# A tuned streaming-encoder layer: low parts of weight blocks kept in DRAM, and score products of both heads in one chain of turns at given places

## The chip, the cores and the metric

The kernel runs on one core of one Trainium2 chip. The metric is the device time of one execution in microseconds, the median of several runs. Five engines work side by side, each through its own queue of instructions in a fixed order: TensorE (PE in the profile), VectorE (DVE), ScalarE (ACT), GpSimd (POOL) and SyncE (SP), which here issues DMAs only. An instruction waits at the head of its engine's queue until its semaphores have come, and all behind it wait too.

## What is computed

One layer on x of 2048 tokens by 1024 features, in float32. h is the normed x, one product with w_in gives the columns of attention, of the recurrent mixer (RWKV-7) and of two gates, and a feed-forward network follows. Cut to what matters here:

```python
proj = h @ w_in[l]
p_att, p_rwkv = proj[..., :ATT_COLS], proj[..., ATT_COLS:ATT_COLS + RWKV_COLS]
p_gate = proj[..., ATT_COLS + RWKV_COLS:] + gate_bias[l]
...
def step(state, inp):
    r_t, w_t, k_t, v_t, aa_t, bb_t = inp
    sa = jnp.einsum('bhij,bhj->bhi', state, aa_t)
    state = (state * w_t[:, :, None, :] + sa[..., None] * bb_t[:, :, None, :]
             + v_t[..., None] * k_t[:, :, None, :])
    y = jnp.einsum('bhij,bhj->bhi', state, r_t)
    return state, y
...
merged = gate_a * (y_a @ proj_a[l]) + gate_b * (y_b @ proj_b[l])
x = x + rms_norm(merged @ w_out[l], post_mix_g[l])
u = jnp.square(jax.nn.relu(hf @ w_up[l])) @ w_down[l]
x = x + rms_norm(u, post_ffn_g[l])
```

There are 8 recurrent heads of 64 features. The kernel does not run the recurrence token by token: it takes chunks of 64 tokens, makes products of all tokens of a chunk with each other (the scores, ps_A), inverts a triangular matrix for each chunk, and carries the state from chunk to chunk.

## The kernel before

The tokens are taken in four groups of 512. Each group goes through `phase_rwkv` (recurrent mixer and gates), `phase_attention` and `phase_merge`; then the feed-forward network runs in two halves. Groups are counted from 0.

**Dense blocks.** A block of 128 columns of w_in is one call of `dense` (L118): the raw block of 512 KB comes on SP (`load_raw`, L64), ScalarE makes its high part whi (L81) and VectorE its low part wlo = raw - whi (L83), both through `wsplit`, with two buffers each. 24 products of 128x512 follow into one bank (psd, L92): eight each of hh x whi, hl x whi and hh x wlo. So the low part is used last. `phase_rwkv` has 30 such blocks a group: 14 of the mixer (columns 12 to 25 of w_in, counted in blocks) and 16 of the gates (26 to 41). The first two blocks of group 0 have their low part made on GpSimd. `follow`, just ahead of it, orders the split behind the emptying of an earlier bank.

**The recurrent stage.** Four pairs of heads, p = 0 to 3, in two batches of two. `rwkv_pre` prepares a pair: r, k, v from dense blocks; ps_z and ps_a (L428, L429) for decay and rate; ps_v, ps_bonus and ps_bk; then the scores. The eight chunks go in two halves of four. Each half takes two banks of PSUM, one for each head (`both`), from a pool of two buffers that ps_z, ps_a, ps_v, ps_bonus, ps_bk and ps_t share. Per chunk and head there is one product (L585). VectorE then empties each bank with four instructions: two into NA (L596), one into AR (L602) and one into BR (L603). NA holds what is to be inverted for two pairs.

`rwkv_inverse` works on VectorE alone: NA is transposed into N (L611), 31 steps of T (L621) and X (L627) follow, and X is transposed (L630) into X1 and XD (L632). `rwkv_blocks` starts TensorE on the result (ps_t, L652 and L660); `rwkv_trans` makes ps_at, ps_w, ps_ug, ps_tq and ps_s, with TQ (L713, L716) and S (L724) by VectorE; `rwkv_chunk` carries the state: ps_st and ps_y on TensorE (L738, L742), ST or, at the last chunk, st on VectorE (L743). `rwkv_post` norms the result: var on VectorE (L756), two steps on GpSimd that end in grs (L757, L759), yn on VectorE (L761). The chunks of the first two pairs run beside the preparation of the other two.

**The order of the work.** A scheduler fills each engine's queue from the program and from the dependences. `queue_behind` adds an order without a wait. The list `self.dl` holds the dense products of the group's `phase_rwkv` in turn (30 x 24), and `place(mm, n)` puts a product behind the n-th of them. Before the change only the first score product of the first pair has a place (SCORES = 150); where the others come is left to the scheduler.

Of the kernel before, what the change touches and what calls it, by code (L numbers as in the profile page):

```python
# [9 lines left out]
F32 = mybir.dt.float32  # L10
BF16 = mybir.dt.bfloat16
F32R = mybir.dt.float32r
# [4 lines left out]
DRAM = bass.MemoryType.DRAM  # L17

P = 128
D = 1024  # L20
KB = D // P
# [15 lines left out]
TURNED = 438  # L37
FIFTH = 494
BONUS = {(0, 1): 138, (1, 0): 258}
SCORES = 150  # L40
TURNS = {1: (588, 592)}
DEC = math.exp(-0.5)

ATT0 = 0
# [12 lines left out]
class Block:  # L57
# [54 lines left out]
    def follow(self):  # L112

        for ins, done in zip((self.high.ins, self.low), self.emptied[-3] if len(self.emptied) > 2 else ()):
            if done is not None:
                self.queue_behind(ins, done.ins)

    def dense(self, col):  # L118

        first = bool(self.raws)  # L120
        wh, wl = self.wsplit(self.w_in(col), "w", KB, P, lower=self.nc.gpsimd if first else None)
        if first:
            n = 1 - len(self.raws)
            self.queue_behind(self.high.ins, self.highs[n])
        self.follow()
        ps = self.pd.tile([P, G], F32, tag="d", name="psd")
        terms = [(wh[:, k], wl[:, k], self.h[0][:, k], self.h[1][:, k]) for k in range(KB)]
        if first:
            pairs = [(u, h) for u, _, h, _ in terms] + [(v, h) for _, v, h, _ in terms] + [(u, l) for u, _, _, l in terms]
            self.mm = [  # L130
                self.nc.tensor.matmul(ps, l, r, start=n == 0, stop=n == len(pairs) - 1).ins
                for n, (l, r) in enumerate(pairs)
            ]
            self.queue_behind(self.mm[0], self.last_transpose)
        else:
            self.mm = self.mm3(ps, terms, True)
        self.dl += self.mm
        return ps
# [19 lines left out]
    def constants(self, ctx, mixing):  # L158
        tc, nc, a = self.tc, self.nc, self.a
        keep = ctx.enter_context(tc.tile_pool(name="const", bufs=1))  # L160
        cp = mixing.enter_context(tc.tile_pool(name="mconst", bufs=1, side="right"))
        dp = ctx.enter_context(tc.tile_pool(name="scratch", bufs=1, space=DRAM))
        nrow = sum(n for _, n in ROWS)
        self.cst = cp.tile([P, nrow], F32, name="cst")
        nc.sync.dma_start(self.cst, a["cst"])
# [279 lines left out]
    def rwkv_pre(self, g, p, rp, NA, between=lambda: None):  # L445
        nc = self.nc
        pc = slice(p * P, (p + 1) * P)
        col = slice(p, p + 1)
# [17 lines left out]
        between()  # L466
        nc.vector.tensor_scalar(tw, tw, -0.5 * DEC, -0.5 * DEC, ALU.mult, ALU.add)
        cum = tw
# [84 lines left out]
        for i, x in enumerate((rh, rl)):  # L553
            mm = nc.tensor.matmul(psb, self.bones, x, start=i == 0, stop=i == 1)
# [22 lines left out]
        for h in range(2):  # L577
            cs = slice(h * 4, h * 4 + 4)

            both = [self.pa.tile([P, 4, P], F32, tag="a", name="ps_A") for _ in range(2)]  # L580
            for j in range(4):
                c = h * 4 + j
                for par, psA in enumerate(both):
                    rw = slice(par * C, par * C + C)
                    mm = nc.tensor.matmul(  # L585
                        psA[:, j].rearrange("p (s t) -> p s t", t=C),
                        BK[rw, c].rearrange("p s t -> p (s t)"),
                        AR[rw, c, par : 3 : 2 - par], start=True, stop=True,
                    )
                    if p == c == par == 0:  # L590
                        self.place(mm, SCORES)
            for par, psA in enumerate(both):
                ow = slice(C - par * C, P - par * C)
                for lo, w in ((0, C), (32, 32)):
                    hw = slice(par * C + lo, par * C + lo + 32)
                    nc.vector.tensor_tensor(  # L596
                        NA[hw, q, cs, 0:w],
                        psA[hw, :, lo : lo + w],
                        n2[hw, cs, par, None].to_broadcast((32, 4, w)),
                        ALU.mult,  # L600
                    )
                nc.vector.tensor_tensor(AR[ow, cs, par], psA[ow, :, 0:C], mS[ow], ALU.mult)  # L602
                nc.vector.tensor_tensor(BR[:, cs, par, 1], psA[:, :, C:P], mN[:, par, cs], ALU.mult)  # L603
# [144 lines left out]
    def rwkv_post(self, p, R):  # L748
# [18 lines left out]
        for h in range(2):  # L767
            ps = self.pr.tile([C, 4, P], F32, tag="wus", name="ps_yt")
            for j in range(4):
                mm = nc.tensor.transpose(ps[:, j], yn[:, h * 4 + j], self.ident)  # L770
                if j == 0 and p in TURNS:
                    self.place(mm, TURNS[p][h])
            cs = slice(h * 4, h * 4 + 4)
# [876 lines left out]
```

## Time and profile before

| | us |
|---|---|
| median of 3 runs | 3199.82 (3198.31 to 3202.85) |
| profiled execution, its own time | 3198.07 |
| its span on the core | 3196.4 |
| TensorE busy | 3147.3 (98%) |
| VectorE busy | 2235.8 (70%) |
| ScalarE busy | 1578.7 (49%) |
| GpSimd busy | 613.8 (19%) |

The mean granted clock of TensorE is 0.999. A row of a timeline is a run of like instructions: start, duration from its first start to its last end, engine, line, operation, tiles (written<-read), shapes and count; in brackets the idle time ahead of it and what ended it. TensorE's instructions overlap, so the time that a run costs is read from its start to the next one's. The trace counts two instructions for a score product. A row of a group has busy time and mean ns of one behind the first bar, and idle time with its releasers behind the second. A row of waits has the waiting engine, tile and line, what it waited for, and total us, times and the longest. A window row has its length, then busy time and count of PE, PEld, DVE, ACT and POOL, the clock, the share of the DMA engines and GB/s.

### The profile page before, as it was taken

The page shows a single profiled execution, that of the slowest core. Times are in us where ns is not written, and L with a number is a line of the kernel's source. Part 1 is how long each engine was busy: PE and PEld are TensorE (multiplying, and loading weights), DVE is VectorE, ACT ScalarE, POOL GpSimd, SP SyncE. Part 2 cuts the span into 40 slices and gives each one's busy share as a digit, 9 for nine tenths or more (in the row PEclk, how much of TensorE's full clock was granted, in tenths as well). Part 3 has the DMA queues.
Part 4 walks back from the last instruction along what each step waited for, and adds up shares of the span by engine and source line. Part 5 has one row for each costly group of instructions (what it writes and reads, how often), then busy time and mean ns, then how long its engine had stood idle before and what let it go on. Part 6 is the DMA issues. An engine that isn't in the chain of part 4 may idle for free. (4 is left out here: it accounts for less than half of the span.)

```text
span 3196.4 us, 49803 instructions
## 1 busy us (share of the span) xinstructions
PE 3147.3 (98%) x18800; PEld 2575.3 (81%) x18800; DVE 2235.8 (70%) x3668; ACT 1578.7 (49%) x2511; POOL 613.8 (19%) x1119
## 2 busy tenths in 40 slices
PE   8999999999999999999999999999999999999998
PEld 6877788778888877888877888888888878888887
DVE  6785667776767786767876776877656768765564
ACT  5435645445745445745534755454544454444343
POOL 3222012132112222112222101221211112210000
PEclk9999999999999999999999999999999999999999
DMA  6245473157573246574236466554877866547565
GB/s 192 86 135 189 134 259 129 60 172 244 175 260 129 77 141 245 186 235 160 94 116 228 160 208 261 192 179 162 293 268 251 281 225 213 170 156 244 191 221 174
DMA packets 197477, 598.82 MB, mean 187 GB/s; under 512 B 25570, under 2 KB 25708, under 8 KB 197236
## 3 DMA queue, kind: packets, MB, share of 16 engines
q1 hardware_dynamic: 139124, 415.24, 40.1%
q0 software_dynamic: 48896, 163.61, 13.6%
q10 hardware_dynamic: 9216, 16.78, 1.4%
q8 instruction: 148, 2.42, 0.3%
q14 instruction: 93, 0.76, 0.1%
HBM read 431.67 MB, written 167.01 MB: 187 GB/s over the span
## 5 line engine op out<-in xcount | busy, mean ns | idle before, releaser
L1469 PE MATMUL ps_dn<-fop 128*128 128x512 f32 x2688 | 610.8, 389 | 0.0
L1469 PEld LDWEIGHTS ps_dn<-fop 128*128 128x128 f32 x2688 | 504.1, 188 | 104.7 <-DVE fop L83 0.2
L81 ACT CAST whi<-wraw 128x1024 fp32r<-128x1024 f32 x232 | 243.5, 1049 | 284.4 <-PE psd L92 202.5
L83 DVE TENSOR_TENSOR wlo<-wraw,whi 128x1024 fp32r<-128x1024 f32 x230 | 280.6, 1220 | 125.4 <-ACT whi L81 80.2
L92 PE MATMUL psd<-hh,whi 128*128 128x512 f32 x1328 | 357.9, 398 | 1.1 <-ACT k L401 1.0
L92 PE MATMUL psd<-hh,wlo 128*128 128x512 f32 x1328 | 356.8, 398 | 0.0
L92 PE MATMUL psd<-hl,whi 128*128 128x512 f32 x1328 | 354.3, 397 | 0.0
L92 PEld LDWEIGHTS psd<-hl,whi 128*128 128x128 f32 x1328 | 243.6, 188 | 47.9
L92 PEld LDWEIGHTS psd<-hh,wlo 128*128 128x128 f32 x1328 | 242.7, 188 | 48.3
L92 PEld LDWEIGHTS psd<-hh,whi 128*128 128x128 f32 x1328 | 241.2, 188 | 50.0 <-ACT k L401 1.6
L83 DVE TENSOR_TENSOR fop<-xraw,fop 128x1024 fp32r<-128x1024 f32 x112 | 137.0, 1223 | 176.2 <-ACT fop L81 175.8
L81 ACT CAST fop<-xraw 128x1024 fp32r<-128x1024 f32 x112 | 117.8, 1052 | 251.0 <-PE ps_dn L1469 191.9
L1339 POOL DMA_DIRECT2D xd<-X x192 | 104.1, 542 | 380.3 <-ACT X L1336 318.2
L83 DVE TENSOR_TENSOR fop<-wdraw,fop 128x1024 fp32r<-128x1024 f32 x112 | 136.6, 1219 | 19.7 <-ACT fop L81 19.4
L81 ACT CAST fop<-wdraw 128x1024 fp32r<-128x1024 f32 x112 | 117.6, 1050 | 35.7 <-DMA wdraw<-in_w_down_dram 22.7
L994 DVE CUSTOM_DVE_ANT_0 sc<-bias,ps_s 128x640 f32<-128x640 f32 (+4 forms) x128 | 93.8, 733 | 39.3 <-PE ps_s L988 23.3
L1012 DVE TENSOR_TENSOR PTl<-ps_pt,PTh 128x640 fp32r<-128x640 f32 (+4 forms) x128 | 94.3, 737 | 27.7 <-ACT PTh L1011 26.8
L1001 ACT ACTIVATE sc<-sc,mn 128x640 f32<-128x640 f32 (+4 forms) x128 | 97.8, 764 | 31.8 <-DVE mn L994 30.4
L81 ACT CAST s12h<-s 128x1024 fp32r<-128x1024 f32 x32 | 33.7, 1053 | 155.5 <-PE ps_u L92 155.5
L92 PE MATMUL ps_p<-yh,whi 128*128 128x512 f32 x256 | 101.7, 400 | 4.9 <-DVE th L1149 2.2
L92 PE MATMUL ps_p<-yl,whi 128*128 128x512 f32 x256 | 101.5, 397 | 0.3 <-DVE yl L83 0.2
L1178 PE MATMUL ps_o<-whi,mh 128*128 128x512 f32 x256 | 100.5, 392 | 0.7 <-DVE o L1189 0.6
(374 smaller groups left out, 6804.0 us busy)
## 6 DMA issues: line engine op xcount, KB each, us to landing
wraw<-in_w_in_dram SPq DMA_DIRECT2D x168, 512.0 KB, 3.7
xraw<-xd SPq DMA_DIRECT2D x112, 512.0 KB, 4.5
xd<-X POOLq DMA_DIRECT2D x192, 256.0 KB, 4.7
wraw<-in_w_up_dram SPq DMA_DIRECT2D x80, 512.0 KB, 4.4
wdraw<-wd SPq DMA_DIRECT2D x64, 512.0 KB, 4.8
wdraw<-in_w_down_dram SPq DMA_DIRECT2D x48, 512.0 KB, 5.0
gd<-gate ACTq DMA_DIRECT2D x64, 256.0 KB, 2.5
wd<-cmb POOLq DMA_DIRECT2D x64, 256.0 KB, 3.7
```

Source lines behind the costliest of these rows:

```text
L81: high = self.high = self.nc.scalar.copy(hi, src)
L83: self.low = lower.tensor_tensor(lo, src, hi.bitcast(F32), ALU.subtract).ins
L92: mm.append(nc.tensor.matmul(ps, l, r, start=n == 0, stop=n == last).ins)
L994: least = nc.vector.tensor_tensor_reduce(sc[:, 0:n], bias[:, s0:640], pss[:, c0 : c0 + n], 1.0, 3.0e38, ALU.add, ALU.min, mn,)
L1001: nc.scalar.activation(sc[:, 0:n], sc[:, 0:n], AF.Exp, scale=-1.0, bias=mn, accum_out=sm[:, col : col + 1])
L1012: nc.vector.tensor_tensor(lv, pst[:, 0:nk], hv.bitcast(F32), ALU.subtract)
L1178: nc.tensor.matmul(ps[t], l[:, k, ts], r[:, k % 2], start=k == 0 and j == 0, stop=k == KB - 1 and j == 2)
L1339: nc.gpsimd.dma_start(self.xd[q][i // 2][:, i % 2], src)
L1469: nc.tensor.matmul(ps, o[:, l, k, sl], o[:, r, k], start=start and n == 0, stop=stop and n == end)
```

## The change

It has two parts.

**Low parts kept.** In group 0 each of the 30 blocks of `phase_rwkv` is split as before, and GpSimd then stores its low part to DRAM (30 stores of 512 KB). In groups 1 to 3 the low part is not computed: SP loads it from DRAM into wlo (90 loads of 512 KB), behind the load of the raw block in the program. ScalarE still makes the high part. The 90 subtractions of VectorE go.

**Scores in chains.** All eight products of a half, both heads in turn, are put into one chain by `queue_behind`, and the first of each half has a place in the list of dense products.

```diff
-SCORES = 150
+SCORES = ((150,163),(266,278),(450,455),(503,511))
+LOWS = range(12, 42)
...
     def dense(self, col):
         first = bool(self.raws)
-        wh, wl = self.wsplit(self.w_in(col), "w", KB, P, lower=self.nc.gpsimd if first else None)
+        kept = self.lows.get(col)
+        if kept is None:
+            wh, wl = self.wsplit(self.w_in(col), "w", KB, P, lower=self.nc.gpsimd if first else None)
+            if col in self.keep_lows:
+                kept = self.lows[col] = self.dp.tile([P, KB, P], F32, name=f"wlow{col // P}")
+                self.nc.gpsimd.dma_start(kept, wl.bitcast(F32))
+        else:
+            raw = self.load_raw(self.w_in(col), KB, P)
+            wh, wl = (self.wp.tile([P, KB, P], F32R, tag="w" + x, bufs=2, name="w" + n) for x, n in (("h", "hi"), ("l", "lo")))
+            self.high = self.nc.scalar.copy(wh, raw)
+            self.low = None
+            self.nc.sync.dma_start(wl.bitcast(F32), kept)
...
             both = [self.pa.tile([P, 4, P], F32, tag="a", name="ps_A") for _ in range(2)]
+            last = None
             for j in range(4):
                 c = h * 4 + j
                 for par, psA in enumerate(both):
...
-                    if p == c == par == 0:
-                        self.place(mm, SCORES)
+                    if last is None:
+                        self.place(mm, SCORES[p][h])
+                    else:
+                        self.queue_behind(mm.ins, last)
+                    last = mm.ins
```

`follow` also skips a low part that is None. Line numbers of the kernel after are one higher from L42 on, 14 higher behind `dense`, and 15 to 18 higher from the scores on: L585 is L600, L596 is L614, L630 is L648, L652 is L670.

The orders of the queues, before and after, at three places. The first is TensorE at the second pair of group 0, before, then after: ps_A are its scores, psd dense products, a count of 4 is one head's half.

```order
L585 MATMUL ps_A<-AR,BK 128x128 x4
L92 MATMUL psd<-hh,wlo 128x512 x2
L585 MATMUL ps_A<-AR,BK 128x128 x4
L92 MATMUL psd<-hh,whi 128x512 x2
L585 MATMUL ps_A<-AR,BK 128x128 x4
L92 MATMUL psd<-hh,whi 128x512 x2
L585 MATMUL ps_A<-AR,BK 128x128 x4
L92 MATMUL psd<-hh,whi 128x512 x4
```

```order
L600 MATMUL ps_A<-AR,BK 128x128 x8
L93 MATMUL psd<-hh,whi 128x512 x5
L93 MATMUL psd<-hl,whi 128x512 x7
L600 MATMUL ps_A<-AR,BK 128x128 x8
L93 MATMUL psd<-hl,whi 128x512
L93 MATMUL psd<-hh,wlo 128x512 x8
```

Before, the four groups of one head each stand two dense products apart; after, two chains of both heads stand twelve apart.

The second is TensorE at the third pair of group 1, before, then after. ps_s, ps_st and ps_y belong to the first batch's chunks (st_101 and st_102 are the states of its two pairs, ps_st<-ST the chunks behind the first).

```order
L723 MATMUL ps_s_6420<-SV,BR 64x64 x16
L585 MATMUL ps_A<-AR,BK 128x128 x8
L92 MATMUL psd<-hh,wlo 128x512 x4
L585 MATMUL ps_A<-AR,BK 128x128 x4
L92 MATMUL psd<-hh,wlo 128x512 x2
L585 MATMUL ps_A<-AR,BK 128x128 x4
L738 MATMUL ps_st<-st_101,TQ 64x64 x2
L742 MATMUL ps_y<-st_101,TQ 64x64 x2
L738 MATMUL ps_st<-st_102,TQ 64x64 x2
L742 MATMUL ps_y<-st_102,TQ 64x64
L428 MATMUL ps_z<-lora,whw 128x512
L429 MATMUL ps_z<-lora,wlw 128x512
```

```order
L93 MATMUL psd<-hh,wlo 128x512 x2
L600 MATMUL ps_A<-AR,BK 128x128 x7
L93 MATMUL psd<-hh,wlo 128x512 x3
L756 MATMUL ps_st<-st_101,TQ 64x64 x2
L760 MATMUL ps_y<-st_101,TQ 64x64 x2
L756 MATMUL ps_st<-st_102,TQ 64x64 x2
L760 MATMUL ps_y<-st_102,TQ 64x64 x2
L600 MATMUL ps_A<-AR,BK 128x128 x8
L756 MATMUL ps_st<-ST,TQ 64x64 x2
L760 MATMUL ps_y<-ST,TQ 64x64 x2
L756 MATMUL ps_st<-ST,TQ 64x64 x2
```

Six dense products stood behind the first half, four ahead of the second half's first head and two between its heads; now three stand behind the first half, and a chunk, then the second half in one chain, then the next chunk; ps_z and ps_a follow two rows further on. Two of the dense products stand inside the first half.

The third is VectorE in group 0, at the end of the first batch's inverse, before, then after. T and X are the inverse's last steps; tk, ta, BK, r and rl belong to the preparation of the second batch, for the same engine.

```order
L621 TENSOR_TENSOR T<-N,X 128x30
L627 TENSOR_TENSOR X<-X,T 128x2x15
L621 TENSOR_TENSOR T<-N,X 128x16
L627 TENSOR_TENSOR X<-X,T 128x16
L630 STREAM_TRANSPOSE X_1227<-X 128x32x16
L520 TENSOR_TENSOR tk<-tk,k 128x512
L632 STREAM_TRANSPOSE XD<-X_1227 128x512
L521 SCALAR_TENSOR_TENSOR ta<-ta,k 128x512
L530 TENSOR_TENSOR BK<-tk,Ei 64x8x64
L527 SCALAR_TENSOR_TENSOR BK<-ta,hkk,Ei 64x8x64 x2
L530 TENSOR_TENSOR BK<-tk,Ei 64x8x64
L533 SCALAR_TENSOR_TENSOR r<-r,cst,tk 128x512
```

```order
L645 TENSOR_TENSOR X<-X,T 128x3x15
L547 SCALAR_TENSOR_TENSOR r<-r,cst,tk 128x512
L639 TENSOR_TENSOR T<-N,X 128x30
L84 TENSOR_TENSOR wlo<-wraw,whi 128x1024
L645 TENSOR_TENSOR X<-X,T 128x2x15
L84 TENSOR_TENSOR rl<-r,rh 128x512
L639 TENSOR_TENSOR T<-N,X 128x16
L416 SCALAR_TENSOR_TENSOR r<-pr,cst,r 128x512
L645 TENSOR_TENSOR X<-X,T 128x16
L648 STREAM_TRANSPOSE X_1251<-X 128x32x16
L84 TENSOR_TENSOR wlo<-wraw,whi 128x1024
L650 STREAM_TRANSPOSE XD<-X_1251 128x512
```

Before, the transpose of X stood ahead of the work for the second batch; after, that work stands between the inverse's steps, and the transpose is behind it. On TensorE in group 0 one more whole dense block (24 products) stands ahead of ps_t than before (dense product 437 instead of 413); in groups 1 to 3 it is at 413 as before.

More of the change, by code (lines that the diff above doesn't have):

```diff
@@ L114, in follow @@
         for ins, done in zip((self.high.ins, self.low), self.emptied[-3] if len(self.emptied) > 2 else ()):
-            if done is not None:
+            if done is not None and ins is not None:
                 self.queue_behind(ins, done.ins)
@@ L161, in constants @@
         cp = mixing.enter_context(tc.tile_pool(name="mconst", bufs=1, side="right"))
-        dp = ctx.enter_context(tc.tile_pool(name="scratch", bufs=1, space=DRAM))
+        dp = self.dp = ctx.enter_context(tc.tile_pool(name="scratch", bufs=1, space=DRAM))
+        self.lows = {}
+        self.keep_lows = {i * P for i in LOWS}
         nrow = sum(n for _, n in ROWS)
```

## The prediction, made before the changed kernel was run

> **What bounds the kernel now.** I read the page first (busy times, costliest groups, DMA issues), then TensorE's list of waits, then the timelines of TensorE and VectorE round the places that the change touches.
>
> ```profile
> PE 3147.3 (98%) x18800; PEld 2575.3 (81%) x18800; DVE 2235.8 (70%) x3668; ACT 1578.7 (49%) x2511; POOL 613.8 (19%) x1119
> ...
> L83 DVE TENSOR_TENSOR wlo<-wraw,whi 128x1024 fp32r<-128x1024 f32 x230 | 280.6, 1220 | 125.4 <-ACT whi L81 80.2
> ...
> wraw<-in_w_in_dram SPq DMA_DIRECT2D x168, 512.0 KB, 3.7
> ...
> wd<-cmb POOLq DMA_DIRECT2D x64, 256.0 KB, 3.7
> ```
> ```profile
> PE ps_st L738 <- DVE ST L743: 4.2, 4, 1.1
> ...
> PE ps_s L723 <- DVE TQ L716: 2.2, 4, 0.9
> ```
> ```profile
> 128.38 1.98 PE L92 MATMUL psd<-hh,wlo 128*128 128x512 f32 x8
> 130.19 1.29 PE L92 MATMUL psd<-hh,whi 128*128 128x512 f32 x5
> ```
>
> TensorE is busy for 3147.3 of 3196.4 us; VectorE has 30% to spare. The two longest waits of the recurrent stage for VectorE are the rows with ST and TQ: 4.2 and 2.2 us in all four groups together. So only two things can move the time by much: less TensorE work, or new waits of TensorE. A dense block is 24 products, of which eight take 1.81 us from one start to the next (128.38 to 130.19), so 0.227 us each and 5.45 us a block.
>
> **The score products.** Here is TensorE at the first pair of the first group, columns start, duration, line, tiles, count; the trace counts two instructions for each product.
>
> ```profile
> 57.26 1.16 PE L585 MATMUL ps_A<-AR,BK 64*128 64x128 f32 x16
> 58.35 0.50 PE L92 MATMUL psd<-hh,whi 128*128 128x512 f32 x1
> ...
> 60.20 1.13 PE L585 MATMUL ps_A<-AR,BK 64*128 64x128 f32 x8
> 61.26 0.73 PE L92 MATMUL psd<-hl,whi 128*128 128x512 f32 x2
> 61.92 1.16 PE L585 MATMUL ps_A<-AR,BK 64*128 64x128 f32 x8
> 63.00 2.12 PE L92 MATMUL psd<-hh,wlo 128*128 128x512 f32 x8
> ```
>
> The first half has both heads in turn: 16 instructions, 1.09 us until the next start (57.26 to 58.35). The second half has the heads one after the other: 8 instructions take 1.06 us (60.20 to 61.26) and the other 8 take 1.08 (61.92 to 63.00). Two heads in turn cost as much as one alone, so a half that is brought into one chain saves 1.07 us. In the order of before, five of the eight halves of a group are split by head (one of the first pair, both of the second, one each of the third and fourth), after the change none. That is 5 x 1.07 = 5.35 us a group, 21.4 us in four groups, off the engine that bounds. This is the gain at its highest; what follows is what the new places take back.
>
> A half goes into two banks, one for each head, and VectorE empties them. The first instruction for each half of the third pair in group 1 (twelve in all, six a half), two of those behind them, and TensorE beside them:
>
> ```profile
> 630.68 0.71 DVE L596 TENSOR_TENSOR NA<-ps_A,n 32x256 f32<-32x256 f32 x2 [0.38 <-PE ps_A L585]
> ...
> 633.76 0.71 DVE L596 TENSOR_TENSOR NA<-ps_A,n 32x256 f32<-32x256 f32 x2
> ...
> 638.12 0.43 DVE L467 TENSOR_SCALAR tw<-tw 128x512 f32<-128x512 f32 x1 [0.73 <-ACT tw L456]
> ...
> 640.86 0.45 DVE L743 SCALAR_TENSOR_TENSOR ST<-ps_st,gC,S 128x64 f32<-128x64 f32 x2
> ```
> ```profile
> 629.49 2.02 PE L585 MATMUL ps_A<-AR,BK 64*128 64x128 f32 x16
> 631.44 1.20 PE L92 MATMUL psd<-hh,wlo 128*128 128x512 f32 x4
> 632.57 1.16 PE L585 MATMUL ps_A<-AR,BK 64*128 64x128 f32 x8
> ...
> 635.40 0.33 PE L738 MATMUL ps_st<-st,TQ 64*64 64x64 f32 x4
> ...
> 636.00 0.50 PE L428 MATMUL ps_z<-lora,whw 128*128 128x512 f32 x1
> ...
> 637.14 0.47 PE L428 MATMUL ps_a<-lora,wha 128*128 128x512 f32 x1 [0.16 <-DVE BR L603]
> ...
> 652.92 0.33 PE L738 MATMUL ps_st<-ST,TQ 64*64 64x64 f32 x4 [1.05 <-DVE ST L743]
> ```
>
> A half takes VectorE 3.08 us (630.68 to 633.76), 1.54 a bank, against 1.09 for TensorE to fill both. A head alone needs one bank at a time and can start on it while the other is still being emptied; heads in turn need both banks from the second product on.
>
> First and second pair: their halves stand 13 and 12 dense products apart (163 - 150 and 278 - 266), 2.95 and 2.72 us, and with the 1.09 of the first half that is 4.04 and 3.81, while the second bank is free 1.09 + 0.1 + 3.08 = 4.27 after the start. Two waits of some 0.2 and 0.4 us: of 3 x 1.07 = 3.2 us, 2.6 a group stay.
>
> Third pair, groups 1 to 3: after the first half come three dense products and one chunk, 1.3 us, and then the second half, which waits for its second bank until 2.4 us after the first half's end (VectorE began 0.76 ahead of that end, 630.68 against 631.44, as before). It ends at 3.4; its two banks are empty at 5.0 and 6.5, and ps_z and ps_a, which take the same two buffers, start then. Before, ps_a stood 5.70 after the same end (631.44 to 637.14). So 0.8 us is lost, while a chunk (636.00 less 635.40, 0.6 us) is sent earlier; the wait of some 0.9 us inside the first half (2.02 against 1.16) is filled by two dense products. Net -0.2. Behind it stand the ST of the next chunks. VectorE has tw, lora_g, k and the scan ahead of the third (638.12 to 640.86 and on), and TensorE now comes to it with fewer products in between: 0.8 us of wait, and the known 1.05 at 652.92 becomes about 1.3. Net -1.1.
>
> Fourth pair, groups 1 to 3: VectorE now has the last chunk, var and yn of the first pair ahead of the first half's evictions, and yn waits for GpSimd.
>
> ```profile
> 669.15 0.68 DVE L756 TENSOR_REDUCE var<-yq 128x8 f32<-128x512 f32 x1
> ...
> 672.90 0.69 DVE L761 TENSOR_TENSOR yn<-ps_y,grs 128x512 f32<-128x512 f32 x1 [1.82 <-POOL grs L759]
> ```
> ```profile
> 666.55 0.20 POOL L757 TENSOR_SCALAR var<-var 128x8 f32<-128x8 f32 x1 [0.55 <-DVE var L756]
> 666.83 1.68 POOL L759 TENSOR_TENSOR grs<-var,nhalf 128x8 f32<-128x8 f32 x1
> ```
>
> GpSimd's two steps take 1.96 us at best (666.55 to 668.51), and from the end of VectorE's second var to its yn it is 3.07 (669.83 to 672.90). I take 2.4. So 0.47 + 0.6 + 2.4 + 0.6, some 4 us, stand between the last chunk and the first eviction, of which two are covered by dense products and the half itself. The second half then waits about 1.8 for its first bank and 0.6 for its second; what it saves is 1.07 and a wait of 0.4. Net -0.9.
>
> Groups 1 to 3 have so far 2.6 - 0.2 - 1.1 - 0.9 = 0.4 us each. A change from dense to small products costs TensorE some 0.2 us (four dense products at 631.44 fill 1.13 us, not 0.91), and about four such changes now lie inside waits: +0.8. The wait of ps_s for TQ (2.2 in four, 0.55 a group) goes for the most part, since the two additions on cmb that VectorE had ahead of TQ no longer stand there: +0.4. I take 1.6 each, 4.8 in three groups. From both sides: -0.5 if no change is hidden and yn takes the 3.07, +3.0 if the evictions start as early as before, so -1.5 to +9.
>
> **The first group** still makes its low parts with VectorE, and VectorE is full there.
>
> ```profile
> 106.00:131.50 25.50, 25.49 (x112) 20.66 (x111) 24.03 (x67) 12.90 (x18) 3.77 (x8) 1.00 0.33 106
> ```
> ```profile
> 130.34 1.15 DVE L630 STREAM_TRANSPOSE X<-X 128x512 f32<-128x512 f32 x1
> 131.35 0.67 DVE L520 TENSOR_TENSOR tk<-tk,k 128x512 f32<-128x512 f32 x1
> 131.94 0.68 DVE L632 STREAM_TRANSPOSE XD<-X 128x512 f32<-128x512 f32 x1
> 132.54 0.66 DVE L521 SCALAR_TENSOR_TENSOR ta<-ta,k 128x512 f32<-128x512 f32 x1
> ...
> 137.29 1.22 DVE L83 TENSOR_TENSOR wlo<-wraw,whi 128x1024 fp32r<-128x1024 f32 x1
> 138.42 0.69 DVE L83 TENSOR_TENSOR rl<-r,rh 128x512 fp32r<-128x512 f32 x1
> 139.03 0.74 DVE L402 SCALAR_TENSOR_TENSOR r<-pr,cst,r 128x512 f32<-128x512 f32 x1
> 139.77 1.23 DVE L83 TENSOR_TENSOR wlo<-wraw,whi 128x1024 fp32r<-128x1024 f32 x1
> ```
> ```profile
> 131.55 1.20 PE L652 MATMUL ps_t<-X,NA 32*32 32x32 f32 x64
> ```
>
> In the window row the fourth number (24.03) is VectorE's busy time in 25.5 us. In the new order tk, ta, the four BK, both r and rl stand ahead of the transpose of X; here they lie behind it, from 131.35 to 139.77 less XD (131.94 to 132.54) and one wlo (137.29 to 138.42), which is 6.7 us. So X comes at 131.5 + 6.7 = 138.2. TensorE sends a whole block more ahead of ps_t (24 x 0.227 = 5.45) and has won 2.6 by then: it is there at 131.55 + 5.45 - 2.6 = 134.4, and waits 3.8 us. That block was the cover between ps_t and the third pair: 43 dense products stood there, now 19. The chain from ps_t over ps_at, ps_w, ps_ug and ps_tq goes through ScalarE and VectorE, so some of the lost cover comes out as waits: none to 5.45, I take 2. The two later pairs save 2.1 and wait for as much and 0.5 more. First group: 2.6 - 3.8 - 2 - 0.5 = -3.7, from -7 (all of the cover lost) to 0 (X in time).
>
> **The low parts.** 90 subtractions of 1220 ns go, 110 us of VectorE, and with them nothing that TensorE waits for but what is in the sums above; by the two rows of waits it could be worth some 6 us at most. 90 loads of 512 KB are added on SP, 30 stores on GpSimd's queue in the first group. A low part is first used 16 products into its block, and its buffer is let go by the block before last, so there are 40 x 0.227 = 9.1 us for a load that takes 3.7. Behind such a load, which waits for its buffer, stand the next raw block and bv on SP; the raw buffers are let go by ScalarE's copy instead of VectorE's subtraction, which is earlier. In the first group GpSimd's store waits for the subtraction; behind it stand the copies of the carry for the next block and var and grs, and the subtraction of the block after next waits until the store has landed. A store of half the size on that queue lands after 3.7 us (wd), so this one after 3.7 to 7.4, also under 9.1. I take 0 for loads and stores; the busiest stretch sets the other end:
>
> ```profile
> 700.00:706.00 6.00, 5.74 (x110) 4.54 (x110) 3.05 (x4) 5.20 (x10) 2.12 (x4) 1.00 0.96 266
> ```
>
> The share of the DMA engines is 0.96 there. One more load for each block, 512 KB in 5.45 us, is 96 GB/s; were it all late, a block would wait for 512 KB at 266 GB/s, 2 us. Over two such blocks in each of three groups that is 12 us.
>
> **Sum.** 4.8 - 3.7 + 0 = 1.1 us faster than the profiled execution, 3198.07 - 1.1 = 3197.0. The median of the runs is 3199.82, 1.75 above the profiled execution, so I forecast 3198.7.
>
> [...]
>
> **The rivals.**
> - Faster: the waits do not come, because TensorE's products between the halves cover the evictions as they do now. For it: TensorE's two longest waits for VectorE in this stage are 6.4 us, and VectorE loses 110 us of work. Against it: the orders, where the covers are gone. Three quarters of the 21.4 us kept, less the first group's 3.7 and 2.6 that it had won, give some -10: 3190; all kept 3178.
> - Slower, the first group's cover: X is not before 138.2, since nothing of its delay is absorbed, and the missing block comes out in full: 3.8 + 5.45 + 0.5 - 2.6 = 7.2 us, with nothing won in groups 1 to 3: 3207. It decides from the point where the groups 1 to 3 win under 0.5 us each. For it: 24.03 of 25.5; against it: the chain behind ps_t has little idle time now.
> - Slower, the low parts come late: 6 blocks x 2 us, 3211. Against it: 9.1 us against 3.7.
> - The change does not do what it says: two heads in turn are no faster in the new chains. Then 21.4 us less are won: 3215 and more. The row at 57.26 speaks against it.
>
> **How the numbers follow.** About 0.2% (6.4 us) is what a measurement of this kernel can tell from no change. The forecast's own band, 3193.4 to 3206.2, has 0.50: the sums of both sides, -1.5 to 9 and -7 to 0, lie mostly inside it. The first rival has 0.28, since my waits rest on orders and could be half as long. The slower ones have 0.12, 0.08 and 0.02. The range leaves out about 0.1 on each side: 3189 to 3210.
>
> **What would show it.** In the profile after: every ps_A row with 16 instructions, or 2 and 14. A wait of ps_t for X of some 4 us near 134 in the first group, and none in the others. Waits of ps_A, ps_z and ps_a for VectorE (BR, NA) of 3 us in all at each third pair; a wait of ps_A at each fourth, with yn ahead waiting for grs. No wait of a dense block for wlo. The forecast is wrong if the waits for VectorE in the groups 1 to 3 come to under 2 us, or if dense products wait for a DMA.

## The result: 0.62% slower, and the profile after

The changed kernel takes 3220.19 us (median of 4 runs, 3213.39 to 3223.39) against 3199.07 us for the kernel before in the same session. The ratio is 1.0062, with a 95% interval of 1.0041 to 1.0083: slower, and outside the predicted range of 3189 to 3210. The profiled execution took 3223.39 us, with a span of 3221.6.

First the busy row of the page and its rows of DMA issues, then the row of the clock:

```profile
PE 3145.9 (98%) x18800; PEld 2568.9 (80%) x18800; DVE 2134.8 (66%) x3578; ACT 1578.5 (49%) x2511; POOL 609.1 (19%) x1149
...
wraw<-in_w_in_dram SPq DMA_DIRECT2D x168, 512.0 KB, 4.2
...
wlo<-wlow SPq DMA_DIRECT2D x90, 512.0 KB, 4.7
```
```profile
core 0: 3221.6 us, clock 0.993
```

VectorE has lost its 101 us of work, and a low part lands 4.7 us after its issue, well inside the 9.1 us that the prediction gave it. The new figure is the clock: 0.993 where it was 0.999. On 3221.6 us the missing 0.007 are worth 22.6 us of full speed, against 3.2 before: 19.4 more. TensorE's list of waits after the change (engine, tile, line, what it waited for; us in all, times, longest):

```profile
PE ps_A L600 <- DVE BR L621: 9.1, 8, 1.3
PE psd L93 <- ACT gate L808: 5.0, 3, 1.7
PE ps_y L760 <- DVE ST L761: 4.5, 4, 1.4
PE ps_z L442 <- DVE BR L621: 3.9, 4, 1.0
...
PE psd L93 <- ACT r L415: 2.4, 1, 2.4
PE ps_a L442 <- DVE BR L621: 2.3, 4, 0.8
...
PE ps_s L741 <- DVE TQ L734: 1.4, 1, 1.4
PE ps_t L670 <- DVE X L648: 1.2, 1, 1.2
```

Of these only ps_a (0.3 us) and ps_s (2.2) stood in the list of before, and the wait for ST stood there at ps_st (4.2). All gaps of TensorE together went from 38.1 to 64.1 us. So the span's 25.2 us are 26.0 of waits and at most 19.4 of clock, less some 20 that is left over for what the chains save (a little less, since a gap inside a half-clock stretch is counted twice). The saving and most of the waits for VectorE were in the prediction; the waits for gate and r, and the clock, were not.

Where the clock goes shows at the third pair of group 1. TensorE's timeline there:

```profile
638.53 0.46 PE L600 MATMUL ps_A<-AR,BK 64*128 64x128 f32 x2
640.05 1.13 PE L600 MATMUL ps_A<-AR,BK 64*128 64x128 f32 x14 [1.07 <-DVE BR L621]
...
642.76 0.77 PE L442 MATMUL ps_z<-lora,whw 128*128 128x512 f32 x1 [0.97 <-DVE BR L621]
643.32 0.63 PE L443 MATMUL ps_z<-lora,wlw 128*128 128x512 f32 x1
644.28 0.77 PE L442 MATMUL ps_a<-lora,wha 128*128 128x512 f32 x1 [0.33 <-DVE BR L621]
...
646.46 3.48 PE L93 MATMUL psd<-hh,whi 128*128 128x512 f32 x8
```

and the windows over it (length, busy time and count of PE, PEld, DVE, ACT and POOL, then the clock, the DMA share and GB/s):

```profile
636.00:640.00 4.00, 2.91 (x35) 2.07 (x33) 3.11 (x9) 0.00 (x0) 0.00 (x0) 1.00 0.26 88
640.00:643.00 3.00, 1.98 (x31) 1.78 (x32) 2.19 (x7) 0.00 (x0) 0.00 (x0) 0.93 0.17 63
643.00:647.00 4.00, 3.67 (x21) 2.16 (x22) 3.15 (x10) 3.00 (x5) 0.00 (x0) 0.50 0.00 0
647.00:649.50 2.50, 2.50 (x7) 1.97 (x6) 1.53 (x4) 2.50 (x6) 1.56 (x3) 0.51 0.26 87
649.50:653.00 3.50, 3.50 (x32) 2.46 (x30) 2.35 (x4) 1.32 (x3) 1.23 (x3) 1.00 0.82 270
```

The three waits of 1.07, 0.97 and 0.33 us are the ones that the prediction placed there. At the end of the second the granted clock falls to 0.50 and stays there until 649.4, with only the wait of 0.33 us left in it: eight dense products, 1.98 us in the rows of before, take 3.48. The half clock lasts 6.83 us (642.6 to 649.4) and costs up to half of that, more than the waits ahead of it.

In the trace of after there are eight such stretches in the recurrent stages, of 3.41 or 6.83 us, 37.5 us in all: two in group 0, and in each later group one at the third pair and one behind the wait of ps_y for ST (1.36 to 1.39 us), 15 to 19 us further on. None follows the waits for gate (1.65 us). Before had none, but for the last 7.9 us of its span (from 3188.45), in which TensorE has no work; after has such an end of 8.8 us (from 3212.84).

In group 0 the waits are other ones. TensorE, then ScalarE, then the window behind:

```profile
130.72 1.97 PE L93 MATMUL psd<-hh,wlo 128*128 128x512 f32 x8
135.07 1.43 PE L93 MATMUL psd<-hh,whi 128*128 128x512 f32 x5 [2.38 <-ACT r L415]
137.65 1.92 PE L670 MATMUL ps_t<-X,NA 32*32 32x32 f32 x64 [1.15 <-DVE X L648]
```
```profile
133.81 0.62 ACT L82 CAST rh<-r 128x512 fp32r<-128x512 f32 x1 [5.89 <-DVE r L547]
134.33 0.68 ACT L415 ACTIVATE r<-psd,omu 128x512 f32<-128x512 f32 x1
```
```profile
137.00:150.00 13.00, 12.24 (x191) 9.35 (x193) 2.29 (x3) 5.69 (x12) 1.94 (x4) 0.74 0.46 155
```

VectorE's r (L547) now stands late, between the steps of the inverse. ScalarE's cast of it waits 5.89 us at the head of its queue, the emptying of the next dense bank (L415) stands behind it, and TensorE waits 2.38 us for that bank, then 1.15 for X, and runs at half clock for 6.83 us behind (137.4 to 144.3). A second stretch of 6.83 us (from 178.4) lies behind the third pair's waits for BR, 0.97 and 1.07 us. By the start of group 0's attention the kernel is 7.4 us behind the one before; each later group adds 5.3 to 5.6, all that follows the last recurrent stage 1.4.

### The profile page after: what moved, and what is told of

The parts are those of the page before. It is cut to its first block, busy times and chain, and to the rows that moved or that the text cites. A ratio compares the mean times of both kernels' runs of the same rounds, so it can differ in the third digit from the quotient of the medians.

```text
span 3221.6 us, 49934 instructions
## 1 busy us (share of the span) xinstructions
PE 3145.9 (98%) x18800; PEld 2568.9 (80%) x18800; DVE 2134.8 (66%) x3578; ACT 1578.5 (49%) x2511; POOL 609.1 (19%) x1149
## 5 line engine op out<-in xcount | busy, mean ns | idle before, releaser
L84 DVE TENSOR_TENSOR wlo<-wraw,whi 128x1024 fp32r<-128x1024 f32 x140 | 170.9, 1220 | 89.7 <-ACT whi L82 59.6
L731 DVE TENSOR_TENSOR TQ<-ps_tq,id 128x256 f32<-128x256 f32 x32 | 13.6, 424 | 138.4 <-PE ps_tq L728 138.4
```

The costliest lines, as they stand in the source:

```text
L84: self.low = lower.tensor_tensor(lo, src, hi.bitcast(F32), ALU.subtract).ins
L731: nc.vector.tensor_tensor(TQ[:, cs, 0], ps[:, :, 0], self.id64[:, None, :].to_broadcast((P, 4, C)), ALU.add)
```

## The experiments

The theories: (a) the chains' saving is real, and is taken back by waits that cost more than themselves, through the clock; (b) waits cost only themselves, and the time is lost in the new transfers; (c) the low parts' removal reorders another engine's queue. Where an expectation speaks of theory one and two, one holds that the waits or the queues' order cost, and two that the transfers do. Medians and ratios are against the kernel before on the same chip. The line numbers of the kernels differ by some 5 to 30.

**One part alone.** First the low parts kept, without chains (the places of before):

```diff
+CHAINED = ()
...
-                    if last is None:
+                    if p not in CHAINED:
+                        if p == c == par == 0:
+                            self.place(mm, 150)
+                    elif last is None:
```

> Low parts kept in DRAM as in the changed kernel, the score products as before. Theory one (the chains of the third and fourth pair make TensorE wait, and TensorE's clock is halved behind these waits): the low parts cost only the new wait for gate, 1.65 us in three groups, so 0 to 6 us slower than before, with the clock at 0.998 or above. Theory two (the low parts' loads and stores are what costs): 12 to 20 us slower.

Measured: 3217.57 us, ratio 1.0061 (1.0047 to 1.0075): alone as slow as the whole change, and in the range that theory two gave, though the trace shows mainly something else. TensorE's waits, and ScalarE ahead of the first of them:

```profile
PE psd L94 <- ACT gate L812: 6.1, 3, 2.1
PE ps_t L682 <- ACT Z L677: 4.4, 5, 2.7
```
```profile
694.13 1.25 ACT L659 COPY XT<-XD 32x512 f32<-32x512 f32 x2 [5.22 <-DVE XD L654]
...
696.55 1.05 ACT L132 CAST whi<-wraw 128x1024 fp32r<-128x1024 f32 x1
697.50 0.68 ACT L812 ACTIVATE gate<-psd,hgb 128x512 f32<-128x512 f32 x1
```

ScalarE at the same place in the kernel before:

```profile
691.68 1.06 ACT L81 CAST whi<-wraw 128x1024 fp32r<-128x1024 f32 x1 [2.53 <-PE psd L92]
697.27 1.24 ACT L637 COPY XT<-XD 32x512 f32<-32x512 f32 x2 [4.53 <-DVE XD L632]
698.54 0.69 ACT L790 ACTIVATE gate<-psd,hgb 128x512 f32<-128x512 f32 x1
```

Before, the cast of the next block's high part stood ahead of the copies that wait for the inverse; now the cast and the emptying of a gate's bank stand behind them, and dense products wait 2.01 to 2.06 us in each of the three groups. No dense product waits for a low part; the queue of another engine has changed. One raw block does come late for what stands behind it. ScalarE in group 2:

```profile
1204.94 1.04 ACT L132 CAST whi<-wraw 128x1024 fp32r<-128x1024 f32 x1 [7.09 <-DMA wraw<-in_w_in_dram]
1206.00 1.18 ACT L677 COPY Z<-ps_t 32x512 f32<-32x512 f32 x2
```

The cast waits 7.09 us for its block, the copy of Z stands behind the cast, and ps_t waits 2.65 us for Z: the longest wait of the second row of the list.

The chains alone, with `LOWS = ()`:

> All chains and places as in the changed kernel, low parts computed as before. Theory one: waits of some 5 us a group at the third and fourth pair and a granted clock of 0.993 to 0.996, so 8 to 18 us slower than before. Theory two: the saving of the chains shows by itself, 10 to 20 us faster than before.

Measured: 3220.03 us, ratio 1.0068 (1.0055 to 1.0082), clock 0.992: 21 us, where theory one gave 8 to 18. With the subtractions still there, what happened in group 0 of the change happens in all four groups: psd waits 2.0 us for r and ps_t up to 1.1 us for X, and over the 100 us that hold these waits and the third pair's the clock is 0.91, 0.97, 0.95 and 0.94 in groups 0 to 3. So the two parts are not additive: each costs what the whole costs, since the low parts take away the late X in groups 1 to 3.

**The first two pairs alone**, without and with low parts (`if p not in CHAINED`: the code of before; `CHAINED = (0, 1)`):

> Chains and places for the first and second pair only, the third and fourth left to the scheduler, low parts computed as before. Theory one: no half clock, three of five halves saved in each group, 3 x 1.07 x 4 = 12.8 us less waits of 1 to 2 us: 8 to 13 us faster than before. Theory two says the same of it. A rival to both, that heads in turn bring nothing: no change.

> As the last one, with the low parts kept in DRAM. Theory one: 3 to 12 us faster than before, clock 0.997 or above. Theory two: slower than before, by 2 to 10 us.

Measured: 3227.62 us, ratio 1.0087 (1.0073 to 1.0101), and 3218.49 us, ratio 1.0060 (1.0047 to 1.0072). Both missed: a gain was expected of each by theory one, and 19 us slower is more than theory two gave the second. The pairs that the prediction thought nearly free of cost are, without the low parts, dearer than all four together. TensorE's dense products get a block ahead of ps_t in every group (place 437 in the list, 413 before), and VectorE, which has the inverse, can't follow: it is busy for 9.44 of the 9.60 us ahead of ps_t in group 1 (600.0 to 609.6). With the low parts the first two pairs change nothing that can be measured (3217.57 against 3218.49).

**Traffic or order.** Both are without chains. In `no_low` the low part is neither made nor loaded in groups 1 to 3 (first diff); the products use the high part in its place, so the low part of w_in is left out of the result there, and the high part is held for 24 products instead of 16. In `extra_copies` everything is as before, and 30 stores and 90 copies of 512 KB from DRAM to DRAM are added, paced behind the raw loads (second diff).

```diff
-            wh, wl = (self.wp.tile([P, KB, P], F32R, tag="w" + x, bufs=2, name="w" + n) for x, n in (("h", "hi"), ("l", "lo")))
+            wh = wl = self.wp.tile([P, KB, P], F32R, tag="wh", bufs=2, name="whi")
             self.high = self.nc.scalar.copy(wh, raw)
             self.low = None
-            self.nc.sync.dma_start(wl.bitcast(F32), kept)
```
```diff
+            wh, wl = self.wsplit(self.w_in(col), "w", KB, P)
+            copy = self.nc.sync.dma_start(self.copies[col], kept).ins
+            self.queue_behind(copy, self.loaded)
```

> Scores as before; in groups 1 to 3 the low part is neither computed nor loaded, and the products with it read the high part in its place, so the result leaves out the low part there. TensorE has as much work as before. Theory one (without the subtractions the queues of VectorE and ScalarE come out in another order, with waits on them that TensorE feels; the loads matter little): 8 to 20 us slower than before, near the 18 of the kernel that only keeps the low parts. Theory two (the loads' traffic on the DMA engines is what costs): no more than 3 us slower than before.

> Scores and low parts as before, and on top the 30 stores of group 0 and, in groups 1 to 3, one copy of 512 KB from DRAM to DRAM behind each raw block on SP that nothing waits for: the traffic of the kept low parts without their part in the queues. Theory one (order of the queues): 0 to 4 us slower than before. Theory two (traffic): 8 to 18 us slower.

Measured: `no_low` 3213.11 us, ratio 1.0046 (1.0034 to 1.0059). Without any load of low parts, and with 100 us less on VectorE, the kernel is 15 us slower, as theory one expected; its list of waits has one new row of weight, for the cast on ScalarE:

```profile
PE psd L94 <- ACT whi L132: 6.4, 3, 2.2
```

In group 1 this cast (694.58) again stands behind the copies XT, which wait 5.32 us for XD, and behind the emptying of a gate's bank.

`extra_copies`: 3209.63 us, ratio 1.0034 (1.0021 to 1.0046), 12 us slower, as theory two expected: the traffic costs too. Its list of waits, and VectorE ahead of one of them:

```profile
PE ps_s L744 <- DVE TQ L737: 7.7, 4, 2.4
```
```profile
1204.15 0.69 DVE L1252 TENSOR_TENSOR cmb<-cmb 128x512 f32<-128x512 f32 x1 [9.48 <-DMA cmb<-in_w_down_dram]
1204.76 0.42 DVE L734 TENSOR_TENSOR TQ<-ps_tq,id 128x256 f32<-128x256 f32 x1
```

The dense blocks do not wait. A load for the feed-forward's weights (cmb) comes late, VectorE's addition on it stands ahead of TQ, the wait for TQ goes from 2.2 to 7.7 us, and the clock over the execution is 0.998 in place of 0.999. The prediction had seen that addition, as something that leaves the place; it had not asked what happens if its load is late.

**The late X.** In `pairs01_x` the first step of VectorE's work for the third pair (tk) is held behind the transpose of X, as in the order of before; in `chains_x` the same is done with all chains. The low parts are computed as before.

```diff
+        tk_ins = nc.vector.tensor_tensor(tk, tk, k, ALU.mult).ins
+        if p == 2:
+            self.queue_behind(tk_ins, self.turned)
```

> Chains for the first two pairs, low parts as before, and VectorE's tk of the third pair held behind the transpose of X by an order, as it stood before the change. Theory (the chains of the first two pairs move VectorE's work for the next batch ahead of X; ps_t waits, and TensorE's clock is halved for 3.4 or 6.8 us behind it): the waits near 137, 609, 1111 and 1609 and the halved clock behind them go, and the 12.8 us of the chains show: 6 to 13 us faster than before. Rival (heads in turn bring nothing, or the order of ps_t is not the cause): 0 to 28 us slower.

> All chains and places as in the changed kernel, low parts as before, VectorE's tk held behind the transpose of X. Theory: of the 21 us that the chains alone cost, the part round ps_t goes, the waits of ps_A, ps_z and ps_a at the third and fourth pair with their halved clock stay: 3 us faster to 10 slower than before. Rival (the third and fourth pair's waits cost no more than themselves, about 5 us a group less 2.1 saved, and the rest lies elsewhere): 12 us slower or more.

Measured: 3209.60 us, ratio 1.0033 (1.0021 to 1.0045), and 3224.34 us, ratio 1.0081 (1.0068 to 1.0093). `pairs01_x` leaves one new wait a group; TensorE's row of group 1, and the windows:

```profile
601.48 1.92 PE L676 MATMUL ps_t<-X,NA 32*32 32x32 f32 x64 [3.37 <-DVE X L654]
```
```profile
594.00:601.00 7.00, 4.10 (x19) 3.06 (x17) 6.56 (x20) 0.59 (x1) 0.44 (x2) 1.00 0.39 114
601.00:608.00 7.00, 6.53 (x76) 4.62 (x76) 5.52 (x8) 4.45 (x7) 1.95 (x2) 0.52 0.10 37
```

VectorE is busy for 6.56 of the 7.00 us ahead (third busy time), so X cannot come sooner: what TensorE wins at the first two pairs it waits for at X. Here a single wait of 3.37 us has a clock of 0.52 over the 7.00 us behind it. Four such waits (13.5 us in all) and a clock of 0.994 over the execution outweigh what the chains save. The expected gain missed. `chains_x` missed its theory too, 26 us slower, which the rival's range takes in: the wait for X is still there (13.5 us in four groups), and the clock over the execution is 0.990, against 0.994 in `pairs01_x`: on 3222.6 us some 13 us of full speed more, about the difference of the two spans (3222.6 and 3210.4). So the rival's reason, waits that cost no more than themselves, does not hold.

**Filling the wait, and moving a block.** `pairs01_fill` is `pairs01_x` with 14 useless dense products sent into ps_t's bank ahead of ps_t; `pairs01_late` instead moves the blocks' start from dense product 412 to 436 in the list.

```diff
+        for i in range(14 if b == 0 else 0):
+            mm = nc.tensor.matmul(ps.rearrange("p q c d -> p (q c d)"), self.bones, self.h[0][:, 0], start=True, stop=True)
```
```diff
-BLOCKS = ((412, 424), (640, 653))
+BLOCKS = ((436, 448), (640, 653))
```

> As the kernel with chains for the first two pairs and tk behind X, and in addition 14 dense products without use (3.2 us, into the bank of ps_t, overwritten by it) right ahead of the first ps_t of each group, in the time in which TensorE waits for X. Theory (the halved clock is the answer to the wait: TensorE had too little to do): the wait is still as long, but filled; the 6.83 us at half clock behind it go, 3.4 us in each of four groups, so 12 to 14 us faster than without these products, 0 to 4 us faster than the kernel before. Rival (the halved clock has another cause, or costs little): within 2 us of the one without, 10 to 14 us slower than before.

> As the kernel with chains for the first two pairs and tk behind X, with ps_t placed behind dense product 436 instead of 412 (the second behind 448), so that blocks' own products stand where TensorE waits for X. Theory: wait and halved clock go without any added work, 27 us in four groups against that kernel, less new waits behind ps_t, whose cover is 13 products less: 0 to 15 us faster than the kernel before. Rival (the chain behind ps_t needs the cover): 5 to 20 us slower than before.

Both missed, theory and rival: 3217.68 us, ratio 1.0062 (1.0049 to 1.0075), and 3242.59 us, ratio 1.0137 (1.0123 to 1.0151). With the filling the wait for X is gone and the next link waits; its list of waits, and the windows where X was waited for and behind the wait for Z in group 1 (at 608.77):

```profile
PE ps_t L694 <- ACT Z L689: 13.3, 8, 3.1
```
```profile
601.00:608.00 7.00, 4.50 (x78) 3.18 (x76) 6.06 (x12) 2.33 (x4) 1.94 (x2) 1.00 0.27 77
608.60:612.00 3.40, 3.23 (x70) 2.88 (x71) 0.37 (x1) 2.67 (x5) 0.19 (x1) 0.67 0.00 0
```

The clock is 1.00 where it was 0.52, and 0.67 behind the wait for Z: in group 1 the lower clock has moved with the wait. With the later block psd waits 6.4 us for r, which ScalarE empties, in each group, and the clock over the execution is 0.989. Neither is a way out: the waits are at another place, and the clock stays under the 0.999 of before (0.996 and 0.989).

**ScalarE's queue put back.** In `lows_act` the low parts are kept, there are no chains, and in groups 1 to 3 ScalarE's copies XT of the second batch are held behind the emptying of the 25th block's bank and the high cast of the 27th. `lows_act_pairs` adds the chains of the first two pairs in groups 1 to 3.

```diff
+            for ins in self.copied[2:]:
+                self.queue_behind(ins, self.acts[24])
+                self.queue_behind(ins, self.casts[26])
```
```diff
-                    if p not in CHAINED:
+                    if p not in CHAINED or g == 0:
```

> Low parts kept, scores as before, and in groups 1 to 3 ScalarE's copies XT<-XD of the second batch held behind the emptying of the 25th block's bank and the high part of the 27th, as in the order of before. Theory (order of ScalarE's queue): the waits for gate, 2.05 us in three groups, and one or two stretches of halved clock go: 6 to 10 us faster than the kernel that only keeps the low parts, 7 to 13 us slower than before. Rival (only the traffic of the loads counts): no faster than that kernel, 15 us slower than before or more.

> As the last one, with the chains of the first two pairs in groups 1 to 3 (group 0, where VectorE still makes the low parts, as before). Theory (with the low parts kept X comes in time, so what the chains save stays): 6 to 10 us faster than the last one, so within 5 us of the kernel before. Rival (the chains save nothing even then): no faster than the last one.

Measured: 3204.16 us, ratio 1.0019 (1.0010 to 1.0029), and 3197.39 us, ratio 0.9996 (0.9987 to 1.0005). Without its waits for gate and Z (6.1 and 4.4 us in the list of `lows_only`, none and 0.2 us here) the kernel with low parts kept is 13 us faster, more than the 6 to 10 expected. ScalarE at the same place, where the gate's bank is now emptied ahead of the copy:

```profile
691.16 0.69 ACT L817 ACTIVATE gate<-psd,hgb 128x512 f32<-128x512 f32 x1
694.20 0.62 ACT L664 COPY XT<-XD 32x512 f32<-32x512 f32 x1 [2.35 <-DVE XD L659]
```

The rest, some 5 us, is in the profiled execution of `lows_act` 2.5 us more gaps than before and a clock of 0.997 in place of 0.999. Its wait of ps_s for TQ is 1.7 us, so the way in which the traffic cost time in `extra_copies` is not seen here.

And with X in time the chains of the first two pairs do bring something, as expected: 6.8 us in three groups, where the prediction's 2.6 a group give 7.8. Some of it may be clock, since the profiled execution of `lows_act` has 0.997 and that of `lows_act_pairs` 0.999.

**The third and the fourth pair.** From this version, which equals the kernel before, the chain of the third pair was added (`CHAINED = (0, 1, 2)`), that of the fourth (`(0, 1, 3)`), and both, always in groups 1 to 3.

> The version with ScalarE's copies held and the chains of the first two pairs in groups 1 to 3, with the third pair's chain added in those groups. Theory (the saving is real, and its return is waits that price themselves and a half clock behind them where they cluster): 1.07 us a group saved, some 2.4 us of waits of ps_A, ps_z and ps_a for VectorE in each of three groups, and behind them a half clock of 3.41 us or more, 1.7 us lost each. That is 0 to 10 us slower than without the third pair's chain, at 3197 to 3207. Rival (waits cost only themselves, as the prediction had it): 1.2 to 2 us a group faster or even, no half clock, 3193 to 3198.

> The same with the fourth pair's chain added instead of the third's. Theory: 1.07 us a group saved against waits of ps_A, ps_y and psd of some 2 to 3 us, and a half clock where they lie within a few us of each other: 3197 to 3205. Rival (waits cost only themselves, and the prediction's -0.9 a group holds): 3199 to 3201, no half clock.

> All four chains in groups 1 to 3, group 0 as before, ScalarE's copies held. Theory: the sum of the two others, 3200 to 3212, with half clock at each third pair; what then lies between it and the changed kernel is the first group and ScalarE's queue. Rival (the third and fourth pairs are not what costs): within 3 us of the version with the first two pairs, 3194 to 3200.

Measured: third 3210.31 us, ratio 1.0034 (1.0022 to 1.0046); fourth 3200.78 us, ratio 1.0008 (0.9999 to 1.0016); both 3208.86 us, ratio 1.0034 (1.0021 to 1.0046). The third pair's chain costs 12.9 us (difference of the medians; the kernel before differs by 0.7 us between the two sessions), more than the 0 to 10 expected and away from the rival. The windows beside it, first without and then with it:

```profile
636.00:646.00 10.00, 9.63 (x86) 7.29 (x87) 7.90 (x18) 7.38 (x14) 3.79 (x7) 1.00 0.42 132
```
```profile
636.00:646.00 10.00, 9.31 (x57) 6.82 (x58) 6.67 (x17) 5.58 (x10) 1.64 (x3) 0.50 0.13 44
```

TensorE is busy for about the same time in both, at half the clock in the second, where it gets through 57 instructions in place of 86. Over the whole run the waits grew by 4.1 us only (42.5 to 46.6 of gaps), the clock went from 0.999 to 0.993, on 3208.5 us some 19 us of full speed (a gap inside the half clock is counted twice): by this estimate nearly the whole price is clock. In group 1 the half clock begins at the wait of 1.07 us (row 635.85; the window from 630.00 to 636.00 has 1.00), ahead of the two others. Theory (b) falls for these 12.9 us, since the loads are the same in both and the waits by themselves are too short. The fourth pair's time lies in the ranges of theory and rival alike. It waits once a group, 4.6 us in all. Behind the wait of 1.52 us in group 1 fourteen instructions of the scores take 1.82 us to the next start, where `lows_act_all` takes 1.07 (670.64 to 671.71), and the clock over the execution is 0.998 in place of 0.999; the rival had no term for the clock:

```profile
662.51 0.46 PE L606 MATMUL ps_A<-AR,BK 64*128 64x128 f32 x2 [1.52 <-DVE BR L630]
662.90 1.20 PE L94 MATMUL psd<-hl,whi 128*128 128x512 f32 x4
664.04 1.89 PE L606 MATMUL ps_A<-AR,BK 64*128 64x128 f32 x14
665.86 2.01 PE L94 MATMUL psd<-hl,whi 128*128 128x512 f32 x4
```

Its price of 3.4 us is 1.1 a group, about as much as such a measurement can tell from nothing. The two don't add: with both, the clock over the execution is 0.996, against 0.993 with the third alone, and the time is no longer.

With all chains in groups 1 to 3 and ScalarE's queue put back the kernel is 0.34% slower, the changed kernel 0.62%. What lies between, some 9 us, is probably group 0's chains (7.4 us behind at its attention) and the gate waits (5.0 us in the list of after); no run takes these two apart. No version is faster than the kernel before by more than can be measured.

## Why the prediction was wrong, point by point

- **The saving of 1.07 us for each split half: about right.** In the trace of after the second half of the first pair takes 1.26 us (61.68 to 62.94, 16 instructions), where its two heads took 1.06 and 1.08. Waits and clock grew by 45 us and the span by 25; the difference is near the predicted 21.4. So the rival that two heads in turn are no faster falls, though its sum (3198.7 + 21.4 = 3220, not 3215) meets the measured time.
- **First and second pair, 2.6 us a group kept: right only with X in time.** Measured 6.8 us in three groups once ScalarE's queue was put back, some of it perhaps clock. In `pairs01_x` the same saving came back whole as a wait of ps_t for X: the sum had taken a gain ahead of VectorE's inverse as a gain at the end.
- **Third pair, groups 1 to 3, "Net -0.2" and "Net -1.1": the step that failed.** Waits of 1.07, 0.97 and 0.33 us are there, at the places and near the size foretold (2.4 us, 3 foretold), and the wait for ST is 1.4 us, where 1.3 was foretold. But they were priced at their own length: the sum has no term for the clock. Measured: -4.3 us a group in place of -1.3, with the clock at 0.993 in place of 0.999.
- **Fourth pair, -0.9: about right, in part by luck.** -1.1 a group, with the wait of 1.5 us in place of 1.8, and a clock of 0.998 in place of 0.999, for which the sum had no term; on top of the third pair's chain it cost nothing.
- **Group 0, -3.7: the wait is right, its place and price are not.** 3.5 us of wait, as against 3.8, but two thirds of it for ScalarE's emptying of r behind its cast of rh. The part of the sum that looked at VectorE's queue did not go on to the queue that waits for it. With two half-clock stretches of 6.83 us, one of them at its third pair, the group loses 7.4 us.
- **The low parts, "I take 0": the other step that failed.** The low parts land in time, as said. But alone they cost 18 us: 13 for the copies XT that moved ahead of the cast and the gate on ScalarE, with the late Z behind (by `lows_act`), and a rest of some 5 whose cause stays open. Traffic alone is large enough (12 us in `extra_copies`, with the late cmb), but its wait for TQ is not seen in `lows_act`. The prediction read the order of TensorE and VectorE and not that of ScalarE, on which it made its claim.

## What to carry to other kernels

Price a new wait of the engine that bounds the kernel by what stands near it: at the third pair 4.1 us of new waits cost 12.9 us of time, so leave the work split where such waits would gather. Ask of each microsecond won whether the next engine in the chain can hand on its result sooner; if it is full, as VectorE was in `pairs01_x` (6.56 of 7.00 us), the gain comes back as a wait (3.37 us there). And when work leaves an engine, read again the queues of all others: what stood behind it may now stand ahead of something that TensorE needs, as the copies XT did in `lows_only` (2.01 to 2.06 us of wait for a gate's bank).

## What the runs showed of the hardware

- In the traces of before and after the granted clock of TensorE is either 1.00 or 0.50. In the trace of after the lower one lasts 6.83 us three times and 3.41 us five times, besides the 8.8 us at the end of the span (7.9 in before). In `lows_act_p012` the clock is 0.50 over the whole window of 10.00 us from 636.00.
- In the trace of after the eight stretches begin at 137.44, 178.40, 642.61, 663.09, 1144.37, 1161.43, 1642.71 and 1659.78 us, which is 12, 136, 6, 141, 5, 141 and 5 times 3.413 us apart.
- In the 3.41 us just ahead of each of these eight TensorE is idle for 1.36 to 1.99 us, some of it in pieces: 1.67 us ahead of 642.61, from the waits of 1.07 and 0.97 us. But 1.65 us of idle time at a gate wait (704.08 to 707.49) and 1.86 us at the wait of ps_o for o (963.46 to 966.87) have a clock of 1.00 behind them. So what decides is not shown; the ends of the products are modelled.
- Waits of like length differ. One of 3.37 us (`pairs01_x`) has a clock of 0.52 over the 7.00 us behind it, one of 1.07 us (`lows_act_p012`, 635.85) a clock of 0.50 over 10.00 us. Behind the gate wait of 2.06 us in `lows_only` eight dense products take 2.36 us to the next start (698.23 to 700.59), in place of 1.81; behind that of 1.65 us in after (704.92 to 706.57) the clock is 1.00. With a wait of 2.4 us of ps_s for TQ the clock over the execution of `lows_act_pairs` is 0.999, as in before, whose longest wait between 30 and 3188 us is 1.30 us (391.08).
